# A seventh pair of split-weight buffers, weight splits on one engine, three blocks by halves, and other banks where stages meet

## The chip, the cores and the metric

The kernel runs on one core of a Trainium2 chip. A core has the engines TensorE (PE, matrix products into eight PSUM banks), VectorE (DVE), ScalarE (ACT), GpSimd (POOL) and SyncE (SP, which only issues DMAs here). They run side by side and wait for one another through semaphores. The metric is the device time of one execution in microseconds; before the change it was 1909.55 us (median of three runs, 1909.32 to 1914.12).

## The reference

Three transformer layers on 512 tokens of width 1024, in two blocks. The first block has a mixer (sliding attention, a state-space mixer and a gated delta rule), an output projection and a gated feed-forward net. The second has two layers, each a mixer, an output projection, and a feed-forward net with a short convolution, with layer norms behind each:

```python
def second_block(x, ...):
    for layer in range(DEPTH_2):
        m = even_mixer(x, ...) if layer % 2 == 0 else odd_mixer(x, ...)
        x = layer_norm(ALPHA * x + m, ln_g[layer, 0], ln_b[layer, 0])
        f = conv_ffn(x, ffn_w_up[layer], ffn_conv_w[layer], ffn_w_down[layer])
        x = layer_norm(ALPHA * x + f, ln_g[layer, 1], ln_b[layer, 1])
```

The even mixer adds two attentions. One of them takes, for each query, only the keys with the highest index scores; these come from index queries and index keys, both projections of x.

## The kernel before

The stages run in this order: block1_mix (to about 284 us), wo1, wf1, even_mix (from about 695), wo2 (from about 952), wf2 (from about 1000), odd_mix (from about 1370), wo3, wf3 (from about 1540). wo1 to wo3 are `project` with `out_proj`, wf1 to wf3 are `ffn`.

**Split products.** Every projection is done in a rounded format with two parts, high and low. A product is three matmuls: high weights by high activations, high by low, low by high. `fm` does one block of 128 output features for all 512 tokens (8 depth steps, 24 matmuls of 512 columns); `tm` and `tm_k` do one tile of 128 tokens. `fm_first` does its blocks by halves of the tokens: first 256 tokens for each of its blocks, then the other 256, so that it can begin before the last two token tiles are there.

**Weights.** `Stream.next` brings 128 x 1024 weights: a DMA from SP's queue into a raw tile (wraw), a cast on ACT (whi), a subtraction (wlo = wraw - whi) on DVE, or on POOL where `tail` is true. Two pools hold them, `cpool` and `wpool`, in turn; each has two wraw tiles and three pairs of whi and wlo. In block1_mix and even_mix there is no wpool, and its room in SBUF belongs to the mixer's own tiles. With `tail` true are the first four weights of each ffn and of odd_mix.

**The border between stages.** A stage ends with four token tiles t = 0 to 3, and `Tail` takes each through the norm: squares on ACT, the root on ACT and its reciprocal on DVE, the scaled x or ty on DVE, then `put_group`: four transposes on PE into a bank of the ring bt, the cast acth on ACT, and actl = bank - acth on DVE. The next stage's matmuls of a token half need acth and actl of its two tiles. Each stage names its PSUM banks in rings (`k.rings`); a block waits until its bank's last reader is done. The order of instructions on each engine is made by a scheduler when the kernel is built; each engine then works through its own list in that order.

The change touches lines 227 to 240 (`Stream.next`), 260, 368 to 375 (`fm_first`), 1103 and 1151 to 1153 (`ffn`), 1175, 1215 and 1369 (`even_mix`: vb is the value tile of its first attention, kh and kl at 1222 the index keys), 1428 and 1462 (`odd_mix`) and 1519 (wo2's banks).

Of the kernel before, what the change touches and what calls it, by code (L numbers as in the profile page):

```python
# [9 lines left out]
F32 = mybir.dt.float32  # L10
F32R = mybir.dt.float32r
# [5 lines left out]
T, D = 512, 1024  # L17
NT = T // 128
# [201 lines left out]
class Stream:  # L220
# [3 lines left out]
    def __init__(self, k, ap):  # L224
        self.k, self.ap, self.off = k, ap, 0

    def next(self, n, tail=False):

        k = self.k
        pool = k.cpool  # L230
        if k.wpool is not None:
            pool = (k.cpool, k.wpool)[k.wturn % 2]
            k.wturn += 1
        raw = pool.tile([128, 1024], F32, name="wraw", bufs=2)[:, :n]
        hi = pool.tile([128, 1024], F32R, name="whi", bufs=3)[:, :n]
        lo = pool.tile([128, 1024], F32R, name="wlo", bufs=3)[:, :n]
        k.nc.sync.dma_start(raw, self.ap[:, self.off:self.off + n])
        self.off += n
        k.split(hi, lo, raw, k.nc.gpsimd if tail else k.nc.vector)
        return hi, lo  # L240


class Kern:
# [15 lines left out]

    def more_weights(self):  # L260

        return self.tc.tile_pool(name="w", bufs=1, reuse_waits="tile")

    def load_consts(self):
# [100 lines left out]
            self.nc.tensor.matmul(ps[:, s], hi[:, k, :], al, start=False, stop=False)  # L365
            self.nc.tensor.matmul(ps[:, s], lo[:, k, :], ah, start=False, stop=(k == nk - 1))  # L366

    def fm_first(self, ws, act, n, ring, tail):

        ps = [self.ps(ring, [128, T]) for _ in range(n)]  # L370
        w = [ws.next(1024, tail) for _ in range(n)]
        for s in (slice(0, T // 2), slice(T // 2, T)):
            for p, v in zip(ps, w):
                self.fm(p, v, act, s=s)
        return ps
# [721 lines left out]
def ffn(k, wname, act, cvec, kind, gi, gj, out=None):  # L1097
# [2 lines left out]
    V, S = nc.vector, nc.scalar  # L1100
    tok = lambda t: slice(t * 128, t * 128 + 128)
    with tc.tile_pool(name=wname, bufs=1, reuse_waits="tile") as P:
        k.rings(h=(0, 1, 2, 3), y=(4, 5, 6, 7), bt=(0, 1))
        ws = Stream(k, k.io[wname])
        ha = k.new_act("A")
        hp = P.tile([128, 2, 3, T], F32R, name="hid", bufs=1)
        tail = Tail(k, P, kind, gi, gj, "bt")
# [40 lines left out]
                for t in range(NT):  # L1148
                    (tail.part if first else tail.more)(t, c, ps[t])

        ps = k.fm_first(ws, act, 4, "h", True)
        hid = [hidden(0, ps[:2]), hidden(1, ps[2:])]
        down(hid + [hidden(f) for f in range(2, 11)], True)
        hid = [hidden(f) for f in range(11, 22)]
        down(hid[:7], False)
        w = [ws.next(1024) for i in range(4)]
        tail.table()
        for t in range(NT):
            for c in range(2):
                ps = k.ps("y", [128, 512])  # L1160
# [8 lines left out]
def even_mix(k, act):  # L1169
# [2 lines left out]
    ctx = ExitStack()  # L1172
    P = ctx.enter_context(tc.tile_pool(name="ev", bufs=1, reuse_waits="tile"))
    V, S, G, E = nc.vector, nc.scalar, nc.gpsimd, nc.tensor
    k.rings(f=(0, 1, 2, 3), g=(0, 1), i=(4, 5, 6, 7), t=(2, 3))
    ws = Stream(k, io["w2"])

    def tile_(shape, name, bufs=1, dt=F32):
        return P.tile(shape, dt, name=name, bufs=bufs)

    tok = lambda t: slice(t * 128, t * 128 + 128)

    def fm_block():
        ps = k.ps("g", [128, T])
        k.fm(ps, ws.next(1024), act)
        return ps
# [15 lines left out]
    p = k.ps("t", [128, 384])  # L1202
# [9 lines left out]


    qs = k.half_act("A", 0)
    for b, p in enumerate(k.fm_first(ws, act, 3, "f", False) + [fm_block()]):
        for i, (q, r) in enumerate(halves):
            o = qs[i][:, b, :]
            S.activation(o[q], p[q], AF.Copy, scale=0.125)
            V.scalar_tensor_tensor(o[r], p[q], 0.125, o[q].bitcast(F32), op0=ALU.mult, op1=ALU.subtract)
    ps = fm_block()  # L1220
# [8 lines left out]
    p = k.ps("t", [128, NT, 64])  # L1229
# [12 lines left out]
    for b in range(4):  # L1242
        p = k.ps("t", [128, 2, 256])
# [6 lines left out]
    p = k.ps("t", [128, 8, NT])  # L1250
# [6 lines left out]
    p = k.ps("t", [128, 128])  # L1257
# [12 lines left out]
    for t in (3, 2, 1):  # L1270
        n = (t + 1) * 128
        work = tile_([128, n], f"work{t}")
        for h in range(8):
            o = qs[h % 2][:, h // 2, tok(t)]
            p = k.ps("i", [128, n])
# [90 lines left out]
    k.open_upper()  # L1366
    k.rings(g=(0,), o=(1,), t=(2, 3), pair=(0, 1))
    mix = {0: k.half_act("A", 0)}
    vb = tile_([128, NT, 512], "vb")
    for b in range(4):  # L1370
        kb = fm_copy("qk", 6)
        qb = fm_copy("qk", 6, 0.125)
# [49 lines left out]
def odd_mix(k, act):  # L1422
# [2 lines left out]
    ctx = ExitStack()  # L1425
    P = ctx.enter_context(tc.tile_pool(name="od", bufs=1, reuse_waits="tile"))
    V, S, G, E = nc.vector, nc.scalar, nc.gpsimd, nc.tensor
    k.rings(g=(0, 1, 2, 3), m=(4, 5), t=(6, 7))
    ws = Stream(k, io["w3"])
    mix = k.new_act("A")  # L1430

# [27 lines left out]
        V.tensor_tensor(d, d, bc(st[:, 2, :]), op=ALU.mult)  # L1459
        G.tensor_tensor(d_, d_, sgug[:, c * 256:c * 256 + 256], op=ALU.mult)  # L1460

    w = [[ws.next(1024, True) for _ in range(2)] for _ in range(2)]
    for t in range(NT):
        for c in range(2):
            k.tm(w[c], act, 256, "g", use_v, [t])
# [32 lines left out]
def body(tc, ctx, io, out):  # L1498
    k = Kern(tc, ctx, io)
    nc = k.nc  # L1500
    act = block1_mix(k)
    k.open_x(ctx)
    for t in range(NT):
        nc.sync.dma_start(k.x[:, t, :], io["x"][t * 128:t * 128 + 128, :])

    def project(name, act, kind, i, j, order=range(KD), y=(0, 1, 2, 3), z=(4, 5), bt=(6, 7)):
        with tc.tile_pool(name=name, bufs=1, reuse_waits="tile") as P:
            k.rings(y=y, z=z, bt=bt)
            ws = Stream(k, io[name])
            return out_proj(k, ws, act, Tail(k, P, kind, i, j, "bt"), order)  # L1510

    with k.more_weights() as k.wpool:
        act = project("wo1", act, "rms", 1, 2, WO1)
        act = ffn(k, "wf1", act, None, "rms", 3, None)
    k.wpool = None
    act = even_mix(k, act)
    with k.more_weights() as k.wpool:
        k.wpool.tile([128, 64], F32, name="wline")
        act = project("wo2", act, "ln", 4, 8, y=(4, 5, 6, 7), z=(0, 1), bt=(2, 3))
        act = ffn(k, "wf2", act, "fcw0", "ln", 5, 9)  # L1520
        act = odd_mix(k, act)
        act = project("wo3", act, "ln", 6, 10)
        ffn(k, "wf3", act, "fcw1", "ln", 7, 11, out)
    k.upper.close()
# [23 lines left out]
```

## Time and profile before

| | us |
|---|---|
| median of the runs | 1909.55 |
| lowest and highest run | 1909.32, 1914.12 |
| the profiled execution | 1915.64 |
| its span, first to last instruction | 1913.9 |
| PE busy | 1846.4 |
| DVE busy | 1078.9 |
| ACT busy | 724.6 |
| POOL busy | 165.0 |

Times in rows count from the start of the span. In a timeline's rows the brackets give how long the engine was idle before the instruction, and what released it. Of two instructions joined in a row (x2) the time is for both. The granted clock of a window (PEclk) is the share of PE's full clock that it had, 1.00 for 2.4 GHz and 0.50 for 1.2 GHz.

### The profile page before, as it was taken

The page shows a single profiled execution, that of the slowest core. Times are in us where ns is not written, and L with a number is a line of the kernel's source. Part 1 is how long each engine was busy: PE and PEld are TensorE (multiplying, and loading weights), DVE is VectorE, ACT ScalarE, POOL GpSimd, SP SyncE. Part 2 cuts the span into 40 slices and gives each one's busy share as a digit, 9 for nine tenths or more (in the row PEclk, how much of TensorE's full clock was granted, in tenths as well). Part 3 has the DMA queues.
Part 4 walks back from the last instruction along what each step waited for, and adds up shares of the span by engine and source line. Part 5 has one row for each costly group of instructions (what it writes and reads, how often), then busy time and mean ns, then how long its engine had stood idle before and what let it go on. Part 6 is the DMA issues. An engine that isn't in the chain of part 4 may idle for free.

```text
span 1913.9 us, 24184 instructions
## 1 busy us (share of the span) xinstructions
PE 1846.4 (96%) x9411; PEld 1531.1 (80%) x9411; DVE 1078.9 (56%) x2094; ACT 724.6 (38%) x1250; POOL 165.0 (9%) x171
## 2 busy tenths in 40 slices
PE   6999999999999989998889999999999999999998
PEld 6889868988888878765578888888898888888886
DVE  7877775433233357984556653664675476625655
ACT  4533344322322235455534432442433344413432
POOL 1403202000000010222120000000210010000000
PEclk9999999999999989999999999999999999999999
DMA  5221024332333222311133323322333333333221
GB/s 171 79 80 37 23 72 150 109 92 85 110 99 93 73 67 81 109 45 34 50 108 126 94 88 110 100 86 90 105 99 88 102 118 95 92 96 109 93 83 45
DMA packets 50131, 171.51 MB, mean 90 GB/s; under 512 B 5912, under 2 KB 7520, under 8 KB 49760
## 3 DMA queue, kind: packets, MB, share of 16 engines
q1 hardware_dynamic: 46848, 161.71, 27.6%
q10 hardware_dynamic: 3168, 8.25, 1.3%
q8 instruction: 74, 1.21, 0.2%
q14 instruction: 41, 0.34, 0.1%
HBM read 167.81 MB, written 2.13 MB: 89 GB/s over the span
## 4 chain that ended last, share of the span: by engine, by line
PE 89%; DVE 4%; ACT 3%; issue 2%; DMA 1%; POOL 1%; SPq 0%; DVEq 0%; ACTq 0%
PE bank L364 17%; PE bank L365 17%; PE bank L366 17%; PE bank L378 10%; PE bank L379 10%; PE bank L380 10%; PE bank L355 1%; PE bank L791 1%; PE bank L1355 1%; DVE wlo L344 1%; PE pair L1321 1%; DMA wraw<-in_w_dram 1%; ACT whi L343 1%; DVE work L1293 1%; DVE m L1292 1%
## 5 line engine op out<-in xcount | busy, mean ns | idle before, releaser
L344 DVE TENSOR_TENSOR wlo<-wraw,whi 128x1024 fp32r<-128x1024 f32 (+3 forms) x279 | 340.8, 1222 | 480.7 <-ACT whi L343 475.6
L364 PE MATMUL bank<-acth,whi 128*128 128x512 f32 (+1 forms) x1552 | 584.3, 378 | 6.5 <-DVE ty L993 2.4
L365 PE MATMUL bank<-actl,whi 128*128 128x512 f32 (+1 forms) x1552 | 583.8, 377 | 2.4 <-DVE actl L344 2.3
L366 PE MATMUL bank<-acth,wlo 128*128 128x512 f32 (+1 forms) x1552 | 583.1, 376 | 0.0
L343 ACT CAST whi<-wraw 128x1024 fp32r<-128x1024 f32 (+3 forms) x295 | 304.0, 1032 | 623.6 <-PE bank L365 321.7
L364 PEld LDWEIGHTS bank<-acth,whi 128*128 128x128 f32 x1552 | 295.0, 191 | 64.3 <-ACT qk L1192 2.8
L365 PEld LDWEIGHTS bank<-actl,whi 128*128 128x128 f32 x1552 | 296.2, 191 | 52.7 <-DVE actl L344 2.9
L366 PEld LDWEIGHTS bank<-acth,wlo 128*128 128x128 f32 x1552 | 296.0, 191 | 51.9 <-issue 1.0
L378 PE MATMUL bank<-whi,acth 128*128 128x512 f32 (+3 forms) x896 | 317.9, 357 | 10.2 <-ACT whi L343 5.7
L379 PE MATMUL bank<-wlo,acth 128*128 128x512 f32 (+3 forms) x896 | 317.4, 354 | 0.0
L380 PE MATMUL bank<-whi,actl 128*128 128x512 f32 (+3 forms) x896 | 316.4, 354 | 0.0
L378 PEld LDWEIGHTS bank<-whi,acth 128*128 128x128 f32 x896 | 171.3, 191 | 36.8 <-ACT whi L343 6.2
L379 PEld LDWEIGHTS bank<-wlo,acth 128*128 128x128 f32 x896 | 171.4, 191 | 23.1
L380 PEld LDWEIGHTS bank<-whi,actl 128*128 128x128 f32 x896 | 171.1, 191 | 22.8
L344 POOL TENSOR_TENSOR wlo<-wraw,whi 128x1024 fp32r<-128x1024 f32 x16 | 39.3, 2472 | 593.3 <-ACT whi L343 590.2
L1115 DVE SCALAR_TENSOR_TENSOR cv<-bank,fcw,cv 128x510 f32<-128x510 f32 x88 | 65.8, 748 | 2.8
L1114 DVE SCALAR_TENSOR_TENSOR cv<-bank,fcw,cv 128x511 f32<-128x511 f32 x88 | 65.4, 743 | 0.0
L1131 ACT ACTIVATE cv<-cv 128x512 f32<-128x512 f32 x44 | 27.8, 633 | 90.4 <-DVE cv L1115 90.4
L343 ACT CAST acth<-cv 128x512 fp32r<-128x512 f32 x48 | 29.7, 620 | 81.0 <-DVE cv L1132 80.6
L1113 ACT ACTIVATE cv<-bank,fcw 128x512 f32<-128x512 f32 x88 | 59.9, 681 | 0.0
L344 DVE TENSOR_TENSOR actl<-bank,acth 128x512 fp32r<-128x512 f32 (+1 forms) x68 | 44.1, 668 | 25.1 <-ACT acth L343 24.8
L343 ACT CAST acth<-bank 128x512 fp32r<-128x512 f32 (+1 forms) x68 | 37.5, 574 | 50.6 <-PE bank L355 38.3
(373 smaller groups left out, 1802.1 us busy)
## 6 DMA issues: line engine op xcount, KB each, us to landing
wraw<-in_wf_dram SPq DMA_DIRECT2D x192, 512.0 KB, 3.5
wraw<-in_w_dram SPq DMA_DIRECT2D x63, 512.0 KB, 3.6
wraw<-in_wo_dram SPq DMA_DIRECT2D x24, 512.0 KB, 3.6
gain<-in_gains_dram ACTq DMA_DIRECT2D x12, 512.0 KB, 4.1
wraw<-in_wf_dram SPq DMA_DIRECT2D x12, 256.0 KB, 2.6
xt<-in_x_dram SPq DMA_DIRECT2D x4, 512.0 KB, 5.3
x<-in_x_dram SPq DMA_DIRECT2D x4, 512.0 KB, 5.8
out_dram<-x SPq DMA_DIRECT2D x8, 256.0 KB, 2.0
```

The source lines that it names most:

```text
L343: self.nc.scalar.copy(hi, src)
L344: (eng or self.nc.vector).tensor_tensor(lo, src, hi.bitcast(F32), op=ALU.subtract)
L364: self.nc.tensor.matmul(ps[:, s], hi[:, k, :], ah, start=(k == 0), stop=False)
L365: self.nc.tensor.matmul(ps[:, s], hi[:, k, :], al, start=False, stop=False)
L366: self.nc.tensor.matmul(ps[:, s], lo[:, k, :], ah, start=False, stop=(k == nk - 1))
L378: self.nc.tensor.matmul(ps, ah, wh, start=first, stop=False)
L379: self.nc.tensor.matmul(ps, ah, wl, start=False, stop=False)
L380: self.nc.tensor.matmul(ps, al, wh, start=False, stop=last)
L1113: S.activation(o, ps, AF.Copy, scale=w(2))
L1114: V.scalar_tensor_tensor(o[:, 1:], ps[:, :T - 1], w(1), o[:, 1:], op0=ALU.mult, op1=ALU.add)
L1115: V.scalar_tensor_tensor(o[:, 2:], ps[:, :T - 2], w(0), o[:, 2:], op0=ALU.mult, op1=ALU.add)
L1131: S.activation(g, g, AF.Silu)
```

## The change

- Each pair of whi and wlo now comes from cpool (three pairs) or wpool (four pairs) in a cycle of seven: c, w, c, w, c, w, w. The raw tiles still alternate. The count starts anew each time wpool is opened.
- `tail` is gone: all weight splits are on DVE. Sixteen were on POOL.
- `ffn` does three blocks by halves and its fourth as a whole, where it did four by halves. Three stages have it, so there are 72 matmuls fewer.
- Banks: ffn's ring h is (1, 2, 3, 0) for (0, 1, 2, 3). In even_mix the first three query blocks are in banks 2 to 4, the fourth in 5, the index keys in 0, transposes in 1 to 3. odd_mix has its first ring in 2 to 5. wo2 has z in 0 and 4 and its transposes in 6 and 7.
- vb is allocated first in even_mix's pool, so it lies at the pool's beginning, where wpool's raw tiles come later.

```diff
-    def next(self, n, tail=False):
+    def next(self, n):
         k = self.k
-        pool = k.cpool
+        load = pool = k.cpool
+        bufs = 3
         if k.wpool is not None:
-            pool = (k.cpool, k.wpool)[k.wturn % 2]
+            load = (k.cpool, k.wpool)[k.wturn % 2]
+            pool, bufs = ((k.cpool, 3), (k.wpool, 4))[(0, 1, 0, 1, 0, 1, 1)[k.wturn % 7]]
             k.wturn += 1
-        raw = pool.tile([128, 1024], F32, name="wraw", bufs=2)[:, :n]
-        hi = pool.tile([128, 1024], F32R, name="whi", bufs=3)[:, :n]
-        lo = pool.tile([128, 1024], F32R, name="wlo", bufs=3)[:, :n]
+        raw = load.tile([128, 1024], F32, name="wraw", bufs=2)[:, :n]
+        hi = pool.tile([128, 1024], F32R, name="whi", bufs=bufs)[:, :n]
+        lo = pool.tile([128, 1024], F32R, name="wlo", bufs=bufs)[:, :n]
...
-        k.split(hi, lo, raw, k.nc.gpsimd if tail else k.nc.vector)
+        k.split(hi, lo, raw)
...
     def more_weights(self):
 
+        self.wturn = 0
...
-    def fm_first(self, ws, act, n, ring, tail):
+    def fm_first(self, ws, act, n, ring):
...
-        k.rings(h=(0, 1, 2, 3), y=(4, 5, 6, 7), bt=(0, 1))
+        k.rings(h=(1, 2, 3, 0), y=(4, 5, 6, 7), bt=(0, 1))
...
-        ps = k.fm_first(ws, act, 4, "h", True)
-        hid = [hidden(0, ps[:2]), hidden(1, ps[2:])]
+        ps = k.fm_first(ws, act, 3, "h")
+        hid = [hidden(0, ps[:2])]
+        p = k.ps("h", [128, T])
+        k.fm(p, ws.next(1024), act)
+        hid.append(hidden(1, [ps[2], p]))
...
-    k.rings(f=(0, 1, 2, 3), g=(0, 1), i=(4, 5, 6, 7), t=(2, 3))
+
+    k.rings(f=(2, 3, 4), g=(5, 0), i=(4, 5, 6, 7), t=(1, 2, 3))
...
+    vb = tile_([128, NT, 512], "vb")
...
-    vb = tile_([128, NT, 512], "vb")
...
-    k.rings(g=(0, 1, 2, 3), m=(4, 5), t=(6, 7))
+    k.rings(g=(2, 3, 4, 5), m=(0, 1), t=(6, 7))
...
-    w = [[ws.next(1024, True) for _ in range(2)] for _ in range(2)]
+    w = [[ws.next(1024) for _ in range(2)] for _ in range(2)]
...
-        act = project("wo2", act, "ln", 4, 8, y=(4, 5, 6, 7), z=(0, 1), bt=(2, 3))
+        act = project("wo2", act, "ln", 4, 8, y=(4, 5, 6, 7), z=(0, 4), bt=(6, 7))
```

The scheduler makes new lists from this. Three places, in each the engine's list before and then now.

DVE at the border from wo1 to wf1, where token tile 1 becomes the lower half of the activations (actl_2986 and actl_2988). Before:

```order
L1054 SCALAR_TENSOR_TENSOR x<-ty,tst,x 128x512 x2
L1060 TENSOR_SCALAR tst<-tst 128x1
L344 TENSOR_TENSOR wlo<-wraw,whi 128x1024
L987 RECIPROCAL tst<-tst 128x1
L344 TENSOR_TENSOR actl_2986<-bank_3055,acth_2985 128x4x128
L344 TENSOR_TENSOR actl_2988<-bank_3063,acth_2987 128x4x128
L1065 SCALAR_TENSOR_TENSOR ty<-x,tst,gain_2785 128x512 x2
```

The same place now:

```order
L1056 SCALAR_TENSOR_TENSOR x<-ty,tst,x 128x512 x2
L346 TENSOR_TENSOR wlo<-wraw,whi 128x1024
L1062 TENSOR_SCALAR tst<-tst 128x1
L346 TENSOR_TENSOR wlo<-wraw,whi 128x1024 x2
L989 RECIPROCAL tst<-tst 128x1
L346 TENSOR_TENSOR actl_2986<-bank_3055,acth_2985 128x4x128
L346 TENSOR_TENSOR actl_2988<-bank_3063,acth_2987 128x4x128
L1067 SCALAR_TENSOR_TENSOR ty<-x,tst,gain_2785 128x512 x2
```

Two splits that stood on POOL's list have joined the one that DVE had in front of actl.

PE at the border from wf1 to even_mix: the end of wf1's last product (bank_5554 before, bank_5530 now), the transposes of tiles 2 and 3 (matmuls by cst), and even_mix's first block (128x256). Before:

```order
L380 MATMUL bank_5554<-whi,hid 128x512
L355 MATMUL bank_5521<-cst,x 128x128 x4
L355 MATMUL bank_5529<-cst,x 128x128 x4
L355 MATMUL bank_5574<-cst,x 128x128 x4
L355 MATMUL bank_5582<-cst,x 128x128 x4
L1203 MATMUL bank_5598<-t_5595,relb 8x384
L364 MATMUL bank_5611<-acth_5410,whi 128x256
L365 MATMUL bank_5611<-actl_5411,whi 128x256
L366 MATMUL bank_5611<-acth_5410,wlo 128x256
```

The same place now (the transposes of tile 3 come 65 rows further down, in the third block):

```order
L382 MATMUL bank_5530<-whi,hid 128x512
L366 MATMUL bank_5588<-acth_5386,whi 128x256
L357 MATMUL bank_5497<-cst,x 128x128 x4
L367 MATMUL bank_5588<-actl_5387,whi 128x256
L368 MATMUL bank_5588<-acth_5386,wlo 128x256
L366 MATMUL bank_5588<-acth_5386,whi 128x256
```

The first block now begins behind wf1's last product, ahead of all four groups of transposes.

ACT at the border from even_mix to wo2: the last copies of the attention (pT), the cast of its result (acth), the table load, and the casts of wo2's weights (whi). Before:

```order
L1344 COPY pT<-bank_7823 128x128
L343 CAST whi<-wraw 128x1024
L1344 COPY pT<-bank_7828 128x128
L343 CAST acth_7243<-bank_7731 128x512
L319 DMA gain_7853<-in_gains_dram 128x1024
L319 DMA gain_7855<-in_gains_dram 128x1024
L979 ACT_TABLE_LOAD
L979 ACTIVATE tsq_7859<-eps_62 128x1
L343 CAST whi<-wraw 128x1024 x6
```

The same place now:

```order
L1353 COPY pT<-bank_7799 128x128
L1353 COPY pT<-bank_7804 128x128
L345 CAST acth_7219<-bank_7707 128x512
L321 DMA gain_7829<-in_gains_dram 128x1024
L321 DMA gain_7831<-in_gains_dram 128x1024
L981 ACT_TABLE_LOAD
L981 ACTIVATE tsq_7835<-eps_62 128x1
L345 CAST whi<-wraw 128x1024 x8
```

The one cast of a weight that stood among the last copies has moved behind the table load, with the others.

## Rows read from the trace of the kernel before

**Rows 1.** The page, parts 1 and 5 (busy, share; count, busy, mean ns).
```profile
PE 1846.4 (96%) x9411; PEld 1531.1 (80%) x9411; DVE 1078.9 (56%) x2094; ACT 724.6 (38%) x1250; POOL 165.0 (9%) x171
L344 DVE TENSOR_TENSOR wlo<-wraw,whi 128x1024 fp32r<-128x1024 f32 (+3 forms) x279 | 340.8, 1222 | 480.7 <-ACT whi L343 475.6
```

**Rows 2.** PE by windows: start:end, length, busy (instructions), clock, DMA share, GB/s.
```profile
345.00:695.00 350.00, 350.00 (x1596) 1.00 0.30 90
329.80:336.00 6.20, 6.14 (x40) 0.72 0.73 233
699.80:710.00 10.20, 9.10 (x37) 0.50 0.57 176
...
710.00:720.00 10.00, 10.00 (x85) 1.00 0.09 31
...
802.40:809.60 7.20, 5.73 (x24) 1.00 0.25 73
...
959.20:966.10 6.90, 5.43 (x13) 0.51 0.52 150
1003.50:1007.10 3.60, 3.53 (x15) 0.53 0.82 287
```

**Rows 3.** Timeline at wo1 to wf1: start, length, engine, line, what, idle before.
```profile
323.01 5.05 POOL L344 TENSOR_TENSOR wlo<-wraw,whi 128x1024 fp32r<-128x1024 f32 x2 [14.79 <-ACT whi L343]
...
326.09 3.06 DVE L344 TENSOR_TENSOR wlo<-wraw,whi 128x1024 fp32r<-128x1024 f32 x1 [2.35 <-ACT whi L343]
...
329.14 1.26 DVE L344 TENSOR_TENSOR actl<-bank,acth 128x512 fp32r<-128x512 f32 x2
329.86 0.39 PE L365 MATMUL bank<-actl,whi 128*128 128x256 f32 x1 [2.35 <-DVE actl L344]
```

**Rows 4.** Timeline at wf1 to even_mix.
```profile
700.05 1.41 DVE L1054 SCALAR_TENSOR_TENSOR x<-ty,tst,x 128x512 f32<-128x512 f32 x2
700.90 1.94 PE L355 MATMUL bank<-cst,x 128*128 128x128 f32 x8 [4.93 <-issue]
```

**Rows 5.** PE's waits: for what, us in total, times, longest.
```profile
PE bank L364 <- ACT qk L1192: 2.0, 2, 1.4
...
PE bank L364 <- DVE actl L1219: 0.9, 1, 0.9
```

**Rows 6.** Timeline in even_mix, where the index keys are copied.
```profile
737.23 0.58 ACT L1224 CAST va<-bank 64x512 fp32r<-64x512 f32 x1
...
738.49 0.42 DVE L1225 CAST va<-va 64x512 fp32r<-64x512 f32 x1
```

**Rows 7.** Timeline at even_mix to wo2.
```profile
952.78 1.28 ACT L979 ACT_TABLE_LOAD   x1 [0.27 <-issue]
953.29 0.50 PE L378 MATMUL bank<-whi,acth 128*128 128x512 f32 x1 [1.40 <-DVE actl L344]
...
954.08 0.20 ACT L979 ACTIVATE tsq<-eps 128x1 f32<-128x1 f32 x1
...
959.57 1.04 ACT L343 CAST whi<-wraw 128x1024 fp32r<-128x1024 f32 x1 [5.29 <-DMA wraw<-in_wo_dram]
...
960.67 2.08 PE L378 MATMUL bank<-whi,acth 128*128 128x512 f32 x4 [5.71 <-ACT whi L343]
```

**Rows 8.** Timeline at wo2 to wf2.
```profile
1000.05 2.78 DVE L344 TENSOR_TENSOR wlo<-wraw,whi 128x1024 fp32r<-128x1024 f32 x1 [2.44 <-ACT whi L343]
...
1003.55 0.58 PE L364 MATMUL bank<-acth,whi 128*128 128x256 f32 x1 [2.44 <-DVE ty L993]
```

**Rows 9.** Timeline at wf2 to odd_mix.
```profile
1372.03 3.46 DVE L1036 SCALAR_TENSOR_TENSOR x<-ty,tst,gain 128x512 f32<-128x512 f32 x2
...
1380.02 1.29 PE L355 MATMUL bank<-cst,x 128*128 128x128 f32 x8 [2.40 <-DVE x L1051]
```

**Rows 10.** Timeline at wo3 to wf3.
```profile
1538.68 3.78 DVE L1051 SCALAR_TENSOR_TENSOR x<-x,tst,gain 128x512 f32<-128x512 f32 x2
...
1543.12 1.11 PE L355 MATMUL bank<-cst,x 128*128 128x128 f32 x4 [2.48 <-DVE actl L344]
```

More of the change, by code (lines that the diff above doesn't have):

```diff
@@ L366, in fm @@
             self.nc.tensor.matmul(ps[:, s], lo[:, k, :], ah, start=False, stop=(k == nk - 1))
-    def fm_first(self, ws, act, n, ring, tail):
+    def fm_first(self, ws, act, n, ring):
         ps = [self.ps(ring, [128, T]) for _ in range(n)]
-        w = [ws.next(1024, tail) for _ in range(n)]
+        w = [ws.next(1024) for _ in range(n)]
         for s in (slice(0, T // 2), slice(T // 2, T)):
@@ L1214, in even_mix @@
     qs = k.half_act("A", 0)
-    for b, p in enumerate(k.fm_first(ws, act, 3, "f", False) + [fm_block()]):
+    for b, p in enumerate(k.fm_first(ws, act, 3, "f") + [fm_block()]):
         for i, (q, r) in enumerate(halves):
```

## The prediction

> **What bounds the kernel now.** I read the page first. TensorE (PE) is busy 1846.4 us of the 1913.9 us span, 96%, and VectorE (DVE) 56% [rows 1]. So time can only come from two places: the gaps of PE, and stretches in which PE works at the lower of its two clocks. I then asked for PE's waits and for the timeline around each long one. Outside the opening, which the change does not touch, the gaps above 2 us lie nearly all where one stage hands over to the next, at six places: wo1 to wf1, wf1 to even_mix, even_mix to wo2, wo2 to wf2, wf2 to odd_mix, wo3 to wf3. Last I asked for the granted clock in windows around these gaps. After each of them the clock is about 0.5, that is 1.2 GHz instead of 2.4 GHz: 0.50 from 699.8 to 710.0, 0.51 from 959.2 to 966.1, 0.53 from 1003.5 to 1007.1; wf2 to odd_mix and wo3 to wf3 have a stretch like the last one, with 3.60 and 3.29 us of PE work at 0.53, and wo1 to wf1 has one inside the row whose mean is 0.72 [rows 2]. What is worked at half clock takes twice as long, so each stretch costs PE's busy time times what the clock lacks: 6.14 x 0.28 = 1.7, 9.10 x 0.50 = 4.5, 5.43 x 0.49 = 2.7, 3.53 x 0.47 = 1.7, and 1.7 and 1.5 at the last two. The gaps and these losses at the six places are what the change can reach, about 24 + 14 = 38 us.
>
> **wo1 to wf1.** GpSimd (POOL) makes two wlo in 5.05 us from 323.01, so until 328.06. DVE's wlo, 1.22 us in the mean [rows 1], starts at 326.09 and takes 3.06; only then does DVE come to the lower half of the activations (actl, 329.14), for which PE stands 2.35 us [rows 3]. After the change the three wlo stand on DVE between the same neighbours. DVE was idle for 2.35 us ahead of its wlo there [rows 3], so two of the three fall into that hole and the third ends 1.22 us after 326.1. The chain then reaches actl at about 328.1 instead of 329.8 with its first result: 1.75 us of the 2.35 go, 0.6 stays. I expect that 0.6 us no longer brings the clock down: behind a wait of 1.4 us in even_mix, which ends at 802.5, it stayed at 1.00 [rows 2, 5]. So 1.7 comes back too. Against it: the transposes of the fourth token tile now come at the very end of the first halves and only four matmuls stand between them and the wait for their actl, so I charge 0.5 us. Sum -2.9; bounds 0 (DVE no earlier) to -4.0.
>
> The Trainium skill (SBUF — State Buffer, section "Who interferes with whom") has it that a VectorE instruction with two SBUF inputs and a GpSimd instruction that reads SBUF exclude each other for a whole instruction. By that rule the DVE split would end at 328.06 + 1.22 = 329.28; the trace has 329.15 [rows 3], so it agrees, and without GpSimd's splits the 1.8 us go. Were the 3.06 us a property of the place and not of the neighbour, this term would be near -0.3, and the three like it below would shrink alike.
>
> **wf1 to even_mix, the largest term.** Before, even_mix's first three banks include the two that hold the transposed tiles, so all eight groups of transposes precede the first matmul. Those of the fourth tile wait for x, whose two halves DVE writes from 700.05 to 701.46, and PE stands 4.93 us until 700.90 and then works at half clock until 710.0 [rows 2, 4]. After, the three blocks lie in banks 2 to 4 and their first halves need only tiles 0 and 1, ready before the gap; they start behind wf1's last matmul, and the fourth tile's transposes come inside the third block, some 8 us later, when x is there. The whole gap goes (4.93), and so do the 4.5 of the clock: -9.4. The bounds are -3 (the second and third block's weights come late, a wait of 2 us stays and the clock falls all the same) and -9.6. The fourth query block gets bank 5 and no longer waits for a bank that is being read, 0.9 us [rows 5].
>
> **The new wait in even_mix.** Before, PE goes from the block that makes the index keys straight into the next projection block (24 matmuls, 5.3 us at 0.219 each, from the first of rows 2). That covers the copies that the index scores need: 0.58 on ScalarE, then 0.42 on DVE [rows 6], and for the lower parts two more on DVE, which I count at 1.1 together. After, the index keys lie in bank 0, which the next block needs too, so the index matmuls come directly behind. PE waits 0.58 + 0.42 and the signals, about 1.1, runs the four matmuls on the upper parts (0.9), and waits some 0.4 more for the lower ones: +1.5, bounds +1.0 and +4 (a DVE split of 1.2 in front and a fall of the clock).
> Behind this the order of blocks, index matmuls and top-k steps shifts through all of even_mix to its end. How its many short waits rearrange I cannot follow: 0, bounds -3 and +3, and I put +2 into the sum, since every projection block now shares one bank earlier than before.
>
> **even_mix to wo2.** Before, the second pool's two raw weight tiles lie over tiles that the attention uses to its end. ScalarE waits 5.29 us for their data; PE stands 1.40 us until 953.29, runs six matmuls and stands 5.71 us until 960.67 [rows 7]. After, vb lies at that address, whose last reader comes a half of even_mix earlier, so the data are there. What comes last then is ScalarE: its cast of the attention result, the table load (1.28 us from 952.78, then 0.20) and one cast of 1.04, so the first matmul can go at 955.3 to 956. PE then stands about 3.8 us where it stood 7.1: -3.3. The gap stays long, so I return only half of the 2.7 of the clock: -1.3. Sum -4.6, bounds -1 (ScalarE later) and -6.
>
> **wo2 to wf2.** DVE's wlo takes 2.78 us at 1000.05 beside GpSimd, and PE waits 2.44 us, here because the second block's bank still holds wo2's output until DVE reads it [rows 8]; the third block's bank is one of the transposes'. After, z is in banks 0 and 4 and the transposes in 6 and 7, so three blocks run in one piece. The first tiles' actl comes some 1.9 us earlier: -1.9, and -1.7 of the clock, +0.2 for the late tile: -3.4, bounds -1 and -4.6.
> **wf2 to odd_mix.** Two steps of x that take 3.46 us together beside GpSimd (1.41 for such a pair in rows 4) delay the fourth tile; PE waits 2.40 [rows 9]. After, the pair is 2.0 shorter, but one or two wlo (1.22) come into the chain, and the first two tiles' blocks in banks 2 to 5 cover it: -1.7 of the wait, -1.7 of the clock: -3.4, bounds 0 and -4.8.
> **wo3 to wf3.** The same pair takes 3.78, PE waits 2.48 [rows 10]. After, 2.3 shorter, one wlo partly in the way, the late tile 0.5: -1.4 and -1.5 of the clock: -2.9, bounds 0 and -4.
>
> **Three blocks by halves.** A block is 24 matmuls of 512 columns (0.219 each, 350.0 / 1596) or 48 of 256 (0.118, 10.0 / 85) [rows 2]: 5.26 against 5.65, so 0.4 for each of three stages: -1.0 with the rounding, bounds 0 and -1.2. The price is cover: the fourth tile's chain has 2.8 us less of other work before it is needed; that is in the terms above. The seventh pair itself removes no wait inside the ffn stages, where PE is never idle (345 to 695 is 350.0 of 350.0 us, [rows 2]): 0. DVE gets 16 x 1.22 = 20 us more work, nearly all beside PE: 0 outside the terms above.
>
> **Sum.** -2.9 - 9.4 - 0.9 + 1.5 + 2.0 - 4.6 - 3.4 - 3.4 - 2.9 - 1.0 = -25.0. The profiled execution was 1915.64 us (span 1913.9), so one of the changed kernel should be near 1891. The runs' median is 1909.55, 6.1 lower than the profiled execution; less 25.0 it is 1884.5. As several terms assume that a shorter gap leaves the clock high, I round to 1886.
>
> **Rivals.**
> A. The gaps shrink, but the clock still falls at the wo and ffn borders, because 0.5 to 1 us of wait is left at two points close together. For it: no row shows how short a wait must be, and waits of 2.4 us were enough. Against it: one of 1.4 us was not [rows 2, 5]. Then four times 1.6 do not come back and wf1 to even_mix keeps half of its 4.5: 1884.5 + 6.5 + 2.2 = 1893.
> B. Nothing to measure: the order of the first blocks was not what PE waited for, the tail's chain through DVE and ScalarE was, and each stage waits later for the fourth tile instead of earlier for the second. For it: PE's waits at four of the borders end with a DVE instruction [rows 3, 8, 9, 10], and three blocks instead of four cover less. Against it: the chain itself gets shorter without GpSimd. Then only even_mix to wo2 (-4.6) and 0.9 + 1.0 remain, with the new waits +3.5: 1907.
> C. Slower: DVE becomes the bound at the borders. All four splits of a stage's start (4 x 1.22 = 4.9 us) queue in front of actl on DVE, where before GpSimd took them. It decides if more than two of them land between a tile's x and its actl: then each of four borders waits 2.5 us longer instead of 1.7 shorter, with the same low clock, and wf1 to even_mix gains nothing as its weights are split late; 1909.5 + 10 + 3.5 - 4.6 = 1918. Against it: DVE's idle time of 2.35 us in front of the wlo [rows 3], and the order, in which at most three come together. The Trainium skill (Perfetto Trace Analysis, section "Optimizing Scalar/DVE Operations") says that handing work from a saturated VectorE to GpSimd can make sense, though the two share a port; by it, taking the work back would be wrong where VectorE is saturated. At 56% [rows 1] it isn't as a whole.
>
> **Chances.** Forecast 0.55 (1877 to 1892), A 0.27, B 0.10, C 0.05, and 0.03 for something slower or equal from even_mix's new order. Within 0.3% (5.7 us) is about what a measurement of this kernel cannot tell from no change. Faster: the first two, some of B: 0.86; same 0.08; slower 0.06. The range of 8 in 10 is 1877 to 1902: all of the forecast, A with its spread, none of C.
>
> **What would show it.** Right: no gap above 1 us between 694 and 704 and the full clock from there to even_mix; the first whi of wo2 near 955; DVE's x pairs at 1.4 to 1.5 us at the borders; gaps of 0.3 to 0.8 us in wf1, wf2 and wf3 at the second halves; a gap of 1 to 1.5 us in front of the index matmuls. Wrong: gaps of 2 us or more, with half clock behind them, at the second halves of the first three blocks (B or C), or a sum of waits inside even_mix that grows by more than 5 us.

## The result, and the profile after

| | before | after |
|---|---|---|
| median of the runs | 1909.95 us (1909.32 to 1914.12, 4 runs) | 1891.41 us (1890.40 to 1893.20, 4 runs) |
| profiled execution, its span | 1915.64, 1913.9 us | 1893.20, 1891.3 us |

The change makes the kernel faster by 1.2%: the ratio is 0.9883, with an interval from 0.985 to 0.9916. (A fourth run of the kernel before has moved its median from 1909.55.) The forecast was 1886, the range 1877 to 1902. First the page of the changed kernel, the rows that answer to [rows 1].

```profile
PE 1835.9 (97%) x9339; PEld 1520.5 (80%) x9339; DVE 1087.2 (57%) x2110; ACT 723.3 (38%) x1250; POOL 122.7 (6%) x155
L346 DVE TENSOR_TENSOR wlo<-wraw,whi 128x1024 fp32r<-128x1024 f32 (+3 forms) x295 | 356.3, 1211 | 457.2 <-ACT whi L345 454.1
```

POOL lost 16 instructions and 42 us, DVE gained 16 splits. PE's busy time fell by 10.5 us although its work is nearly the same: that is work now done at full clock. The windows of PE show it; they answer to [rows 2].

```profile
326.00:333.00 7.00, 6.37 (x48) 1.00 0.64 225
...
696.00:706.00 10.00, 10.00 (x85) 1.00 0.39 114
...
727.90:731.30 3.40, 3.40 (x12) 0.50 0.31 118
...
949.80:953.20 3.40, 3.37 (x9) 0.50 0.65 189
1003.00:1007.00 4.00, 4.00 (x36) 1.00 0.25 75
1369.60:1373.00 3.40, 3.40 (x19) 0.50 0.00 0
1543.00:1547.00 4.00, 4.00 (x20) 1.00 0.71 240
```

From 696 to 706, where PE stood 4.93 us before and then worked at half clock, it is now busy for 10.00 of 10.00 us at full clock. wo1 to wf1, wo2 to wf2 and wo3 to wf3 keep the full clock as well. Even_mix to wo2 and wf2 to odd_mix still have a stretch at 0.50, and there is a new one at 727.9.

Next the timeline of the changed kernel at wo1 to wf1, in answer to [rows 3]. The columns are start, length, engine, line, what, and the idle time before.

```profile
326.30 1.22 DVE L346 TENSOR_TENSOR wlo<-wraw,whi 128x1024 fp32r<-128x1024 f32 x1 [0.31 <-ACT whi L345]
...
327.52 1.27 DVE L346 TENSOR_TENSOR actl<-bank,acth 128x512 fp32r<-128x512 f32 x2
...
328.25 0.39 PE L367 MATMUL bank<-actl,whi 128*128 128x256 f32 x1 [0.64 <-DVE actl L346]
```

The third split takes 1.22 us instead of 3.06 and actl starts at 327.52 instead of 329.14; with a wait of 0.23 just before it, 0.87 us of the 2.35 are left.

The stretch in even_mix where the index keys are copied, in answer to [rows 6]:

```profile
723.51 1.04 ACT L345 CAST whi<-wraw 128x1024 fp32r<-128x1024 f32 x1 [1.10 <-DMA wraw<-in_w_dram]
...
724.58 0.58 ACT L1233 CAST va<-bank 64x512 fp32r<-64x512 f32 x1
724.58 1.22 DVE L346 TENSOR_TENSOR wlo<-wraw,whi 128x1024 fp32r<-128x1024 f32 x1 [1.45 <-ACT whi L345]
...
725.84 0.42 DVE L1234 CAST va<-va 64x512 fp32r<-64x512 f32 x1
...
726.32 0.50 PE L1285 MATMUL bank<-va,acth 128*128 128x512 f32 x1 [3.05 <-DVE va L1234]
```

The two copies still take 0.58 and 0.42 us. But a weight cast stands in front of the first on ACT, and behind the late cast comes a split in front of the second on DVE. PE waits 3.05 us, where I had put 1.5.

Even_mix to wo2, in answer to [rows 7]; ACT's line is read first:

```profile
946.28 1.28 ACT L981 ACT_TABLE_LOAD   x1 [0.27 <-issue]
...
947.68 1.98 ACT L345 CAST whi<-wraw 128x1024 fp32r<-128x1024 f32 x2
...
948.76 0.96 PE L380 MATMUL bank<-whi,acth 128*128 128x512 f32 x3 [3.38 <-ACT whi L345]
```

The first casts no longer wait for data: table load, a small step, cast, first matmul, as forecast. Last, wf2 to odd_mix, in answer to [rows 9]:

```profile
1359.21 1.41 DVE L1038 SCALAR_TENSOR_TENSOR x<-ty,tst,gain 128x512 f32<-128x512 f32 x2
...
1361.90 1.42 DVE L1053 SCALAR_TENSOR_TENSOR x<-x,tst,gain 128x512 f32<-128x512 f32 x2
...
1365.80 1.04 PE L357 MATMUL bank<-cst,x 128*128 128x128 f32 x8
...
1366.43 0.58 ACT L345 CAST acth<-bank 128x512 fp32r<-128x512 f32 x1 [4.76 <-PE bank L357]
...
1367.04 1.28 ACT L1457 ACT_TABLE_LOAD   x1
...
1368.33 1.21 ACT L1457 ACTIVATE v<-bank 128x256 f32<-128x256 f32 x4
...
1368.77 0.39 PE L380 MATMUL bank<-whi,acth 128*128 128x256 f32 x1 [1.93 <-ACT v L1457]
```

The x pair takes 1.41 instead of 3.46 and PE's wait for it is gone, but another has come: four banks hold the first two tiles' blocks, and ACT empties the first only after its cast of the fourth token tile, which itself waits 4.76 us for the transposes, and a table load. The transposes are not late because of x, which is ready at 1363.32: they stand on PE's list behind all of the first two tiles' blocks, which end at 1365.80.

Added up, place by place: all of PE's idle time, plus half of its busy time at half clock. The last row is PE's busy time without that half.

| place | before, us | after, us | forecast | measured |
|---|---|---|---|---|
| wo1 to wf1 | 2.4 + 1.7 | 0.9 + 0 | -2.9 | -3.2 |
| wf1 to even_mix | 4.9 + 4.6 | 0 + 0 | -9.4 | -9.5 |
| inside even_mix | 17.7 + 3.4 | 22.4 + 5.0 | +2.6 | +6.3 |
| even_mix to wo2 | 7.3 + 2.7 | 3.4 + 1.7 | -4.6 | -4.9 |
| wo2 to wf2 | 3.4 + 1.7 | 0.2 + 0 | -3.4 | -4.9 |
| wf2 to odd_mix | 3.2 + 1.7 | 1.9 + 1.7 | -3.4 | -1.3 |
| wo3 to wf3 | 2.5 + 1.6 | 0.2 + 0 | -2.9 | -3.9 |
| work at full clock | 1824.27 | 1822.85 | -1.0 | -1.4 |

The sum is -22.8; the spans differ by 22.6. (The opening and the end of the kernel, which are not in the table, differ by 0.2.)

### The profile page after: what moved, and what is told of

It is laid out like the page before. It is cut to its first block, busy times and chain, and to the rows that moved or that the text cites. A ratio compares the mean times of both kernels' runs of the same rounds, so it can differ in the third digit from the quotient of the medians.

```text
span 1891.3 us, 24031 instructions
## 1 busy us (share of the span) xinstructions
PE 1835.9 (97%) x9339; PEld 1520.5 (80%) x9339; DVE 1087.2 (57%) x2110; ACT 723.3 (38%) x1250; POOL 122.7 (6%) x155
## 4 chain that ended last, share of the span: by engine, by line
PE 92%; DVE 3%; ACT 3%; DMA 1%; issue 1%; POOL 0%; SPq 0%; DVEq 0%; ACTq 0%
PE bank L366 17%; PE bank L367 17%; PE bank L368 17%; PE bank L380 11%; PE bank L381 11%; PE bank L382 10%; DMA wraw<-in_w_dram 1%; PE bank L357 1%; PE bank L1364 1%; PE pair L1330 1%; PE bank L793 1%; ACT whi L345 1%; DVE wlo L346 1%; DVE work L1292 0%; PE bank L1350 0%
## 5 line engine op out<-in xcount | busy, mean ns | idle before, releaser
L346 DVE TENSOR_TENSOR wlo<-wraw,whi 128x1024 fp32r<-128x1024 f32 (+3 forms) x295 | 356.3, 1211 | 457.2 <-ACT whi L345 454.1
L366 PE MATMUL bank<-acth,whi 128*128 128x512 f32 (+1 forms) x1528 | 576.9, 380 | 5.6 <-ACT qk L1201 4.1
L367 PE MATMUL bank<-actl,whi 128*128 128x512 f32 (+1 forms) x1528 | 577.6, 379 | 0.6 <-DVE actl L346 0.6
L368 PE MATMUL bank<-acth,wlo 128*128 128x512 f32 (+1 forms) x1528 | 577.0, 378 | 0.0
L366 PEld LDWEIGHTS bank<-acth,whi 128*128 128x128 f32 x1528 | 287.4, 189 | 62.0 <-ACT qk L1201 5.0
L367 PEld LDWEIGHTS bank<-actl,whi 128*128 128x128 f32 x1528 | 288.6, 189 | 54.4 <-issue 1.8
L368 PEld LDWEIGHTS bank<-acth,wlo 128*128 128x128 f32 x1528 | 288.7, 189 | 52.6 <-issue 1.0
L1130 DVE TENSOR_TENSOR cv<-cv,bank 128x512 f32<-128x512 f32 x22 | 15.1, 687 | 73.8 <-PE bank L368 73.1
L382 PE MATMUL bank<-whi,hid 128*128 128x512 f32 x144 | 56.3, 391 | 0.0
```

The costliest lines, as they stand in the source:

```text
L346: (eng or self.nc.vector).tensor_tensor(lo, src, hi.bitcast(F32), op=ALU.subtract)
L366: self.nc.tensor.matmul(ps[:, s], hi[:, k, :], ah, start=(k == 0), stop=False)
L382: self.nc.tensor.matmul(ps, al, wh, start=False, stop=last)
```

## The experiments

Each kernel's median stands against the kernel before on the same chip: 1915.19 us for e1 to e4, 1915.46 for e5 and e10 to e12, 1920.51 for e6, e7, e15 and e16. The changed kernel was not run again beside them. One kernel's executions scatter by up to 1%, and the granted clock goes with it: on the chip of e6 the kernel before took from 1906.38 us, at a mean clock of 0.990, to 1925.52, at 0.981. So where less is in question the rows of the trace decide.

**e2: the engine of the splits.** Sixteen splits are back on GpSimd; banks and halves stay. One place of the edit:

```
...
-        w = [ws.next(1024) for _ in range(n)]
+        w = [ws.next(1024, ring == "h") for _ in range(n)]
...
```

> The changed kernel, with the sixteen weight splits back on GpSimd. Theory 1 (part of the gain at four borders is that DVE is no longer held up by GpSimd): DVE's instructions beside a split take 2.5 to 3 us again, PE waits 1.5 to 2.5 us at wo1 to wf1, wf2 to odd_mix and wo3 to wf3, with half clock behind them: 1896 to 1902 us. Rival (the banks and the order of the blocks give the whole gain, and the splits' engine does not matter): DVE's instructions are stretched all the same, but PE works beside them: 1890 to 1893 us.

1892.12 us, ratio 0.9885 (0.9849 to 0.992): no difference from the change. The timeline of e2 at wo1 to wf1:

```profile
324.64 2.69 POOL L346 TENSOR_TENSOR wlo<-wraw,whi 128x1024 fp32r<-128x1024 f32 x1 [14.79 <-ACT whi L345]
...
326.15 3.39 DVE L346 TENSOR_TENSOR wlo<-wraw,whi 128x1024 fp32r<-128x1024 f32 x2 [0.79 <-ACT whi L345]
...
330.26 0.38 PE L367 MATMUL bank<-actl,whi 128*128 128x256 f32 x1 [1.25 <-DVE actl L346]
```

Beside GpSimd's split, two of DVE take 3.39 us instead of 2.4, so that effect is real; but PE's gap is 1.25 us here, not 2.35, the clock stays up, and wf2 to odd_mix even waits only 0.4, without half clock behind it: there a part of the last block stands behind the transposes on PE's list and covers them. Taking the splits from GpSimd is worth nothing that can be measured. At the borders to the three ffn stages this leaves the banks, since the number of blocks by halves (e6) makes no difference either; but no run puts the banks of ffn and wo2 back alone, so there the cause is argued and not shown.

**e3: even_mix's banks alone put back.**

```
-    k.rings(f=(2, 3, 4), g=(5, 0), i=(4, 5, 6, 7), t=(1, 2, 3))
+    k.rings(f=(0, 1, 2, 3), g=(0, 1), i=(4, 5, 6, 7), t=(2, 3))
```

> The changed kernel, with even_mix's banks as before (first blocks in 0 to 2, fourth in 3 or 0, keys behind it). Theory 1 (these banks gain 9.5 us at the border from wf1 and cost 6.3 us inside even_mix): PE waits 4.9 us near 700 again with 10 us of half clock behind it, and the 3.05 us wait before the index matmuls is gone: about 1894.5 us, 3 above the changed kernel. Rival (the even_mix banks are worth their 9.5 us, and the longer waits inside even_mix come from something else, the added DVE splits or the later DMAs): about 1901 us.

1902.89 us, ratio 0.9937 (0.9915 to 0.996), some 10 us above e2 and e4 on the same chip; the rival's time. PE's waits in e3's even_mix:

```profile
PE bank L357 <- issue: 4.9, 1, 4.9
...
PE bank L366 <- DVE actl L1228: 0.9, 1, 0.9
```

The 4.9 and the 0.9 are back to the tenth and no key wait is left. By the medians this one line of banks gives about half of the whole gain, net of the key wait that it makes. By the rows it is less: from 300 us on, idle time and lost clock come to 66.2 us before, 50.8 in e3 and 45.3 in the change, about a quarter of the gain. A part of e3's distance lies where the change does nothing, in the opening, whose instructions are the same. First e3, then the changed kernel:

```profile
156.30:176.80 20.50, 20.50 (x93) 0.50 0.01 3
```

```profile
156.30:176.80 20.50, 20.23 (x164) 1.00 0.18 53
```

In all, half clock cost e3's profiled execution 15.1 us in the opening, and the change's 4.7.

The rival was also right that the longer waits inside even_mix come from something else than these banks. Without the key wait and the 0.9 they come to 17.0 us before, 19.4 in the change, and 20.4 in e3 with the old banks. The longest of them in e3:

```profile
852.22 0.51 ACT L1343 ACTIVATE lg<-lg,ast 128x256 f32<-128x256 f32 x1 [1.43 <-DVE ast L1341]
...
853.66 0.57 ACT L1201 COPY qk<-bank 128x512 f32<-128x512 f32 x1
...
854.29 0.50 PE L366 MATMUL bank<-acth,whi 128*128 128x512 f32 x1 [2.89 <-ACT qk L1201]
```

The copy that frees PE's bank stands on ACT's list behind an exponential that waits for DVE, and a weight cast; in the kernel before, the same copy (843.72) stood ahead of that exponential (845.88). It is the new order of ACT's list that makes this wait.

**e1: cover for the key copies.** The index keys are moved from bank 0 to bank 5, so that a projection block can run ahead of the index scores.

```
-    k.rings(f=(2, 3, 4), g=(5, 0), i=(4, 5, 6, 7), t=(1, 2, 3))
+    k.rings(f=(2, 3, 4), g=(0, 5), i=(4, 5, 6, 7), t=(1, 2, 3))
```

> The changed kernel, with the index keys in bank 5 and the fourth query block in bank 0 (the other way round than in the change). Theory 1 (the wait before the index matmuls is a bank conflict): the next projection block stands behind the index keys again and covers their copies, so the 3.05 us wait at 726 and the half clock behind it (1.7 us) go, and the border from wf1 to even_mix stays without a wait: about 1886.5 us, 4.8 below the changed kernel's 1891.4. Rival (the block only lends its cover, and the wait comes back later, where that block now covers other waits of even_mix): 1890 to 1892, with the sum of waits in even_mix as in the changed kernel (22 us).

1895.40 us, ratio 0.9899 (0.9864 to 0.9935): not faster. The key wait is gone (the index matmuls follow the block at 727.40), but other waits have grown. e1's timeline:

```profile
809.55 0.55 PE L1350 MATMUL bank<-cst,lg 128*128 128x128 f32 x3 [1.69 <-ACT pT L1353]
...
836.51 0.90 PE L1350 MATMUL bank<-cst,lg 128*128 128x128 f32 x3 [3.26 <-ACT pT L1353]
```

PE idles 21.8 us between 718 and 942, against 22.4 in the change: the cover was only lent, as the rival had it.

**e11, e12: half of the top-k rounds.** Both run 8 of the 16 rounds (the selection is then another one), e12 with e1's banks as well.

```
-            for _ in range(16):
+            for _ in range(8):
...
```

> The changed kernel with 8 instead of 16 rounds of the top-k selection per tile (half of DVE's selection work in even_mix is left out, some 23 us of DVE, none of PE). Theory 2 (in the middle of even_mix DVE is the bound, and the waits of PE there are DVE's queue): PE's waits between 718 and 852 fall from 13.6 us to the 3 us in front of the index matmuls and a few more, below 8, and the time by 5 us or more: 1880 to 1886. Theory 1 (they are bank waits): they stay at 12 us or more, and the time at 1889 to 1893.

> The same with half of the top-k rounds left out, and the index keys in bank 5 and the fourth query block in bank 0. Theory 2: now that DVE has room, covering the index keys' copies is worth what it says, 3.05 us and the half clock behind it: 3 to 5 us below the run with 8 rounds and the change's banks. Rival (the cover is lent in any case): within 1.5 us of that run.

One execution each: 1888.93 and 1884.13 us. The longest of PE's waits from 718 to 852, of e11:

```profile
PE bank L1285 <- DVE va L1234: 2.8, 1, 2.8
```

Taking 22 us of work from DVE in this stretch (116.0 to 94.0 us) leaves e11 with 11.9 us of idle PE, against 13.6: the forecast of under 8 missed, and both numbers lie at the edge of what Theory 1 had (12 or more, 1889 to 1893). With the banks of e1 it is 8.8, and e12 is 4.8 us below e11. So in these two executions the key wait goes for nothing once the rounds in front of the attention's steps on DVE are shorter. How much time that saves, single executions can't tell: half clock inside even_mix alone costs e11 3.4 us more than e12.

**e16: the same room on DVE without leaving work out.** e1's banks, six banks for odd_mix's v (e15 below), and the softmax's division on ACT.

```
...
-                V.tensor_scalar(lg, lg, st[:, i, 2:3], None, op0=ALU.mult)
+                S.activation(lg, lg, AF.Copy, scale=st[:, i, 2:3])
...
```

> The changed kernel with three edits: banks 0 and 5 in turn for even_mix's projections, so that a block covers the copies of the index keys; the six banks for v in odd_mix; and the division by the softmax's sum (64 steps, 416 ns each on DVE, 26 us) on ScalarE, which was in line for DVE there. Theory (inside even_mix DVE's steps end the chain, and the cover that the first edit lends fails only for that): the key wait of 3.05 us with its half clock (3.9 together) and the 3.6 at odd_mix go, DVE's room keeps the other waits of even_mix from growing: 1891.4 - 3.9 - 3.6 = 1884 (ratio 0.984). Rival (ScalarE takes DVE's place: its exponentials, its copies of the transposed shares and the division are one line, 64 x 0.56 us more): even_mix's waits move to ScalarE and grow by 4 us or more, 1888 to 1893.

1893.00 us, ratio 0.9876 (0.9843 to 0.991): the rival's time, at its upper edge. PE idles 23.1 us between 718 and 942. The longest wait in e16's timeline:

```profile
809.81 0.41 DVE L1302 MATCH_REPLACE8 work<-m,work 128x256 f32<-128x256 f32 x1
...
810.14 0.41 DVE L1341 CUSTOM_DVE_ANT_0 lg<-pair,acth 128x256 f32<-128x256 f32 x1
...
810.59 0.51 ACT L1343 ACTIVATE lg<-lg,ast 128x256 f32<-128x256 f32 x1 [3.27 <-DVE ast L1341]
...
813.22 0.57 ACT L1201 COPY qk<-bank 128x512 f32<-128x512 f32 x1
...
813.84 0.80 PE L366 MATMUL bank<-acth,whi 128*128 128x512 f32 x1 [5.64 <-ACT qk L1201]
```

DVE is busy 138.2 us from 718 to 942 instead of 160.4, but the step that ACT waits for (L1341) stands behind top-k rounds all the same, and the copy that frees PE's bank stands behind exponentials, a division and a weight cast on ACT. It is the order in the two lines, and not only DVE's load, that ends this wait; for the shorter ones that is not shown.

**e4, e10, e7: what lets wo2's weights go early.** e4 puts the line of vb back from even_mix's beginning to the attention; e10 is the kernel before with that line at the beginning and nothing else; e7 is the change with three and three split pairs (its diff).

```
-            pool, bufs = ((k.cpool, 3), (k.wpool, 4))[(0, 1, 0, 1, 0, 1, 1)[k.wturn % 7]]
+            pool, bufs = ((k.cpool, 3), (k.wpool, 3))[k.wturn % 2]
```

> The changed kernel, with vb allocated late as before. Theory 1 (where vb lies sets when wo2's raw weights can come): ScalarE waits about 5 us for wo2's second weights and PE stands 7 us instead of 3.4 near 950, with 7 us of half clock: about 1896 us, 5 above the changed kernel. Rival (ScalarE's list sets it: the cast behind the table load comes late in any case): 1890.5 to 1892.5 us.

> The kernel before, with vb allocated first and nothing else changed. Theory 1 (vb's place alone lets wo2's weights come early): the raw weights' DMAs go out near 930 instead of 951, ScalarE's wait of 5.29 us goes, PE stands about 3.5 us instead of 7.1 near 950 to 960: 4 to 5 us below the kernel before. Rival (something else of the change did it, vb's place alone does nothing, as putting it back did nothing): the same time as the kernel before, within 2 us, and the 5.7 us wait stays.

> The changed kernel with three and three split pairs in turn instead of three and four, all else as changed. Theory (the seventh pair sets the order of SP's list of DMAs, not vb's address): with six pairs one raw tile of wf2, which waits until DVE has split a weight of wo2, stands on SP ahead of wo2's last two weights, as in the kernel before; these then land late at even_mix to wo2, PE's last wait there is 4 to 6 us instead of 3.38, with a longer half clock, and the time is 3 to 5 us above the changed kernel's: 1895 (ratio 0.990). The prediction's cause (vb's address alone lets the weights go): the wait stays near 3.4 us and the time at 1891 (ratio 0.988). In either case a wait at the other borders that is new would be the seventh pair's own share.

e4: 1892.21 us, ratio 0.9882 (0.9848 to 0.9915), PE's wait 3.60 instead of 3.38. e10: 1914.00, ratio 1.0006 (0.998 to 1.0032), PE's wait 4.75 instead of 5.71. e7: 1897.11, ratio 0.9893 (0.9859 to 0.9927), PE's wait 4.65. SP's line tells the three apart. A group's length runs from the issue of its first DMA to that of its last. First the changed kernel:

```profile
923.87 0.33 SPq L238 DMA_DIRECT2D wraw<-in_wf_dram  x1
924.24 27.21 SPq L238 DMA_DIRECT2D wraw<-in_wo_dram  x4
```

e10, with vb first but the rest as before:

```profile
929.94 21.44 SPq L237 DMA_DIRECT2D wraw<-in_wf_dram  x2
951.43 12.78 SPq L237 DMA_DIRECT2D wraw<-in_wo_dram  x4
```

e7, with vb first and the change's banks, but six pairs:

```profile
925.52 21.38 SPq L238 DMA_DIRECT2D wraw<-in_wf_dram  x2
946.96 9.14 SPq L238 DMA_DIRECT2D wraw<-in_wo_dram  x4
```

With six pairs a second weight of wf2 stands on SP ahead of wo2's last weights. It waits some 21 us for a raw tile that DVE frees by a split, and everything behind it waits too. With the seventh pair it stands behind them, and two of the four weights go at 924. In e4 wo2's weights go at 940.66 and still land before the cast behind the table load, so vb's place matters little as long as SP's order is right. ACT and PE of e7 at this place:

```profile
951.43 1.04 ACT L345 CAST whi<-wraw 128x1024 fp32r<-128x1024 f32 x1 [1.06 <-DMA wraw<-in_wo_dram]
...
952.53 1.04 PE L380 MATMUL bank<-whi,acth 128*128 128x512 f32 x2 [4.65 <-ACT whi L345]
```

The cast waits for data again, but for 1.06 us, since here the table load (to 950.2) hides most of it. So the seventh pair is worth 1.3 us of PE's time at this border, less than the 3 to 5 that I expected. PE's idle time here, 7.3 us before and 3.4 in the change, is 6.3 with vb first alone (e10) and 4.8 in e7: of the 3.9 us, vb's place takes 1.0, the seventh pair 1.4, and the remaining 1.5 no run separates. The rest of e7's distance is inside its interval and inside a longer half clock behind the key wait (6.8 us instead of 3.4), which I can't put down to the pairs.

**e6: four blocks by halves.** As the kernel before has them.

```
-        ps = k.fm_first(ws, act, 3, "h")
...
+        ps = k.fm_first(ws, act, 4, "h")
...
```

> The changed kernel with four blocks by halves at the beginning of wf1, wf2 and wf3 instead of three. Theory (the third of the prediction's small terms: halves cost PE 0.4 us a stage and cover the fourth tile): PE's busy time grows by 1.2 us, the wait of 0.87 us at wo1 to wf1 goes (with it nothing of the clock, which stays high there), so 1891 to 1892, no difference to be measured; in the profile no wait above 0.3 us at these three borders. Rival (the late tile was not what the 0.87 us waited for): the wait stays, 1892.6. Second rival (the fourth block needs a bank that is still being read): a wait of 1.5 us or more with half clock behind it at one of the three borders, 1894 or more.

1892.73 us, ratio 0.9883 (0.9847 to 0.992): no difference. PE's idle time at wo1 to wf1 is 0.52 us instead of 0.87, where I expected none above 0.3, at the other two borders 0.24 instead of 0.20. PE's work at full clock, counted as in the table, is 2.3 us more, where 1.2 was expected; some of that is the scatter of this count (1820.8 to 1824.0 over eight other profiles with three blocks by halves).

**e5, e15: the new wait at odd_mix.** e5 gives odd_mix's projection blocks six banks in turn throughout; e15, whose diff stands here, does so for the four blocks of v and goes back to four banks behind them.

```
+    k.rings(g=(2, 3, 4, 5, 6, 7))
...
+    k.rings(g=(2, 3, 4, 5), m=(0, 1), t=(6, 7))
```

> The changed kernel, with odd_mix's first ring in six banks, 2 to 7, instead of four, 2 to 5. Theory 1 (the new wait of 1.93 us at 1369 is the fifth block's wait for a bank, which the first block's Gelu on ScalarE frees late because ScalarE stands in line behind a cast that waits for the fourth tile's transposes): the wait goes, with the half clock behind it: 3.6 us below the changed kernel's profile, that is 1887 to 1889 us. Rival (ScalarE's line itself is late, and the next blocks wait for something else of it): a wait of 1 to 2 us stays between 1360 and 1375, 1890 to 1893 us.

> The changed kernel with six banks (2 to 7) in turn for odd_mix's four blocks of v, and the changed kernel's four banks (2 to 5), transposes in 6 and 7, from there on. Theory (the wait of 1.93 us at wf2 to odd_mix is for a bank that ScalarE still reads, and the one of 2.55 us that a run with six banks throughout had came from the transposes of the later part sharing banks 6 and 7): both are away, and the half clock of 3.4 us behind the first: 1.93 + 1.7 = 3.6 less, 1888 (ratio 0.986). Rival (the wait is ScalarE's lateness and only moves on): a wait of 1.5 us or more comes elsewhere in odd_mix, 1891 (ratio 0.988).

e5: 1896.61 us, ratio 0.9912 (0.988 to 0.9943), above what either theory had. The 1.93 are gone, but the transposes that share banks 6 and 7 pay for it, with half clock behind them:

```profile
1435.16 1.25 PE L357 MATMUL bank<-cst,oc 128*128 128x128 f32 x8 [2.55 <-DVE actl L346]
```

e15: 1888.71 us, ratio 0.9859 (0.9823 to 0.9895). PE in e15, from 1366 to 1374:

```profile
1366.00:1374.00 8.00, 8.00 (x69) 1.00 0.01 2
```

No wait, full clock, and no new wait up to the end: the 3.6 us of that border are there. Five of its six executions (1886.92 to 1889.28) are below all four of the changed kernel, the sixth is 1900.30; the medians differ by 2.7 us, and the intervals of the two ratios overlap. By its rows e15 beats both kernels, by the runs alone it is likely and not settled.

## Why the prediction was right, and where it was not

The main step held: the three first blocks lie in banks that do not wait for the fourth tile's transposes, and the 9.4 us forecast at wf1 to even_mix are 9.5. With these banks put back alone (e3) the wait is back. The three borders to an ffn followed, and a rest of 0.2 to 0.9 us did leave the clock high there, which was the doubt behind rival A. Rivals B and C fell: the late tile costs at most 0.87 us at these three, and nothing at wf1 to even_mix. But my reason against A, that a wait of 1.4 us leaves the clock high, did not hold in the trace that I had. Behind a wait of 1.41 us that ends at 882.11, the kernel before has half clock from 884.1 to 887.5:

```profile
882.00:888.00 6.00, 5.22 (x16) 0.72 0.28 89
```

Four steps did not hold as written.

- **GpSimd as the cause.** Several terms were worked out from splits and x pairs that get shorter without GpSimd. They did (1.22 for 3.06, 1.41 for 3.46). By the rule of the Trainium skill (SBUF — State Buffer, "Who interferes with whom") they should, and e2's 3.39 us for two splits beside GpSimd agrees with it (by the rule they would end at 324.64 + 2.69 + 2.44 = 329.77, and they end at 329.54). But with GpSimd's splits back e2 is as fast: PE has other blocks to work on meanwhile.
- **Even_mix to wo2.** The size was right (-4.9 for -4.6) and the cause wrong in the main, so the size is luck. vb's place alone takes 1.0 us of PE's idle time and nothing measurable of the time (e10); SP's line, which the seventh pair reorders, takes 1.4 (e7), and the table load hides a good part of a late weight as well (e4, e7). Where the rest comes from stays open. I had costed the seventh pair at 0, looking only inside the ffn stages, and not followed SP's line across the stage's end.
- **The key wait** is the mis-sized term: 3.05 us and 1.7 of the clock, 4.8 instead of 1.5 and above the upper bound of +4, because of a weight cast that I had not counted and the split that the bound had named. The other waits of even_mix grew by some 2.4, as the +2.0 had it, but not for the reason given, the shared bank: with the old banks (e3) they grew by more. Together, waits grew by 4.7 us inside even_mix, close to the 5 that I had named as a sign of being wrong.
- **Wf2 to odd_mix.** The wait for x went, and a bank wait took its place: -1.3 for -3.4. I had counted the blocks that the four banks hold as cover, and not asked when ACT, behind a cast and a table load, empties the first of them, nor where PE's list has the transposes. e15 shows that the bank was what PE waited for: with six banks the border costs nothing.

The sum missed by 2.4 us (-25.0 against -22.6). It is better than its terms: two came out 5.8 us worse than forecast and the others 3.6 better, which is luck. That the forecast lies 5.4 us under the median has another source too: -25.0 was worked out on an execution of 1915.64 us and taken off a median of 1909.55, while the profiled execution of the changed kernel lies only 1.8 above its median. Those 4.3 us belong to the scatter of one kernel's executions (rounding 1884.5 up to 1886 took 1.5 off the distance).

Open stays what sets even_mix's many short waits: the old banks do not bring them back to their old size (e3), shorter top-k rounds with e1's banks take some of them away (e12), moving the division does not (e16), and no run changed the order of steps on DVE and ACT alone.

## What to carry to other kernels

At a border of stages, ask first which bank the next blocks lie in and who empties it last; the engine that prepares the weights matters only if PE is still waiting for it after that. Follow every in-order line across the border, the DMA issuer's among them: one transfer that waits for its tile holds back all behind it, here for 21 us. And where a wait is covered by a block, the block is taken from somewhere else: look for the wait that it covered there.

## What the runs showed of the hardware

Whether the clock falls behind a wait is not read from the wait's length. In the change a wait of 1.41 us at 876.56 is followed by half clock and one of 2.86 at 821.82 is not; in e15, whose code is the same up to odd_mix, the key wait of 2.96 us is followed by full clock, and the 2.87 us at 821.56 by half. PE in the changed kernel:

```profile
821.80:825.20 3.40, 3.38 (x18) 1.00 0.38 94
...
878.10:881.50 3.40, 3.14 (x8) 0.50 0.55 154
```

and in e15:

```profile
727.90:731.30 3.40, 3.40 (x16) 1.00 0.43 149
821.80:825.20 3.40, 3.40 (x13) 0.58 0.43 122
```

So in these runs a wait of 1.4 to 3.4 us costs its length, and behind it nothing, 1.7 us or up to 3.4 more (e4 and e7, 6.8 us of half clock behind a key wait of 2.80 and 2.97), and which it is can differ between executions.
